# Row loads a step ahead, the readout's scratch in another buffer, and modulation sums on ScalarE in a two-layer hybrid block

## The chip, the core and the metric

The kernel runs on one core of a Trainium2 chip. The metric is the device time of one execution in microseconds. PE is the matrix engine, ACT the scalar engine, DVE the vector engine, POOL the GpSimd engine, SP the engine whose queue issues most of the DMAs.

## What is computed

Two layers over 768 tokens (256 of context, 512 latent), model width 1024. In each layer a conditioning vector gives shift, scale and gate by one product with `ada_w`. The normalised input goes through one wide projection `w_in`; three token mixers (a bidirectional RWKV-7 recurrence, a latent attention, a windowed attention) read slices of it, are gated, projected and merged.

```python
def trunk_layer(x, xc, c, c_ctx, ada_w, ada_b, norm_g, w_in, ...):
    mod = jax.nn.silu(c) @ ada_w + ada_b
    mod_c = jax.nn.silu(c_ctx) @ ada_w + ada_b
    ...
    h = rms_norm(x, norm_g) * (1.0 + scale) + shift
    za, ga, zb, gb, zc, gc, zg = jnp.split(h @ w_in, list(IN_CUTS), axis=-1)
    ...
    ya, yac = rwkv7_branch(za, zac, ...)
...
def rwkv7_scan(r, decay, k, v, kk, a, s0, reverse):
    def step(S, inp):
        r_t, w_t, k_t, v_t, kk_t, a_t = inp
        sa = jnp.einsum('bhvk,bhk->bhv', S, kk_t)
        S = (S * w_t[:, :, None, :] - sa[..., None] * (kk_t * a_t)[:, :, None, :]
             + v_t[..., None] * k_t[:, :, None, :])
        return S, jnp.einsum('bhvk,bhk->bhv', S, r_t)
...
def rwkv7_readout(y, r, v, k_dir, r_k, gn_g, gn_b, dtype):
    mu = jnp.mean(y, axis=-1, keepdims=True)
    var = jnp.mean(jnp.square(y - mu), axis=-1, keepdims=True)
    yn = ((y - mu) * lax.rsqrt(var + A_GN_EPS)).reshape(B, T, BRANCH_WIDTH) * gn_g + gn_b
    ...
```

## The kernel before

**The recurrence.** Time is cut into 12 chunks of 64 tokens; 8 heads times 2 directions run together. For chunk i, `rwkv_scores` (L619) loads from DRAM the update rows `BK` (3 buffers) and `AR` (4 buffers) and the values `UV` (4 buffers), multiplies them on PE (`scps`), masks the products on DVE into `AR` and `TR` (L656, L658), and transposes `BK` on PE. `rwkv_step` (L719) applies one chunk to the state: `Rp`, `Up`, `Sp`, `Yp` on PE, with copies and sums on ACT and DVE between them (`UV`, `So`, `yo`).

**The inversion.** For each group of four chunks, `rwkv_inverse` (L668) inverts the unit triangular 64 by 64 blocks. Four loads bring `TT` (L674, L675; one buffer). DVE transposes it into `inv` (L681), POOL writes a mask into `YB` (L684), then 30 pairs of DVE instructions solve the 32 by 32 halves (L690, L692), each pair using the result of the one before, and two more transposes (L695, L696) end the part on DVE. Only then can PE do the off-diagonal products `zp` and `yp`. There are three inversions to a layer. The first has to be done before chunk 0; the second and third run beside the chunks of the group ahead of them.

**The readout** (L578) normalises finished tokens. Its scratch `ro` has six planes of 256 columns and the tag `AR`, so it takes one of the four `AR` buffers for as long as it lasts. The squares go to planes 4 and 5 in turn.

**The modulation.** `ada` (L227) multiplies the conditioning vectors by blocks of `ada_w` into a PSUM bank `modps`. DVE copies the bank into `row` (L269), PE adds the four partial rows with `sum4` back into the same bank, and DVE adds the bias into `mod` (L277 or L280). Blocks with a weight pool of their own are 512 wide and come at the very start; the other 16 blocks are 256 wide and are spread over layer 0: 4 for layer 0's gate, 12 for layer 1.

**Fillers.** Between the steps of the recurrence the function `pace` puts pieces of other work on PE: projections of `w_in` (`g`) and the `ada` blocks. A projection's weights `wf` are loaded by SP (L165), cast by ACT into `wh` (L168), and POOL makes the rest `wl` (L169); its result in PSUM is finished by ACT (tanh into `st`, L791) and, for a gate projection, by DVE (L793), and SP stores it to `gd` (L795).

**What sets the order.** A list scheduler gives every engine its order when the program is built; each engine then runs its instructions strictly in that order, and SP issues its DMAs in that order too. Priorities are set by `band`. Inside `in_line` PE's order is the order in which the code was written, so PE's order in the recurrence is by hand; the orders of SP, DVE, ACT and POOL come from the scheduler. In `rwkv` (L521) the scores of chunks 0 and 1 and the loads of the first inversion are put in first; step i then puts in the scores of chunk i+2, loads and all.

Of the kernel before, what the change touches and what calls it, by code (L numbers as in the profile page):

```python
# [19 lines left out]
P = 128  # L20
# [40 lines left out]
def build(tc, A, out):  # L61
# [165 lines left out]
    def ada(l, pp, mod, parts, pool=None):  # L227
# [30 lines left out]
        for i_, (q, h) in enumerate((q, h) for q in parts for h in range(512 // n)):  # L258
            ps = bank(i_)

            for k0 in range(0, KT, 4):
                with band(SERVE):
                    ws = four(q, h, k0)
                    for i in range(4):
                        mm(ps[32 * i:32 * i + 32], sc2[:, k0 + i, :], ws[i], start=(k0 == 0), stop=(k0 + 4 == KT),
                           skip_group_check=True)
                yield
            row = spool.tile([P, T], F32, tag="st", name="row", bufs=2)
            V.tensor_copy(row[:, 0:n], ps)  # L269
            nf = n // P  # L270
            pt = ps[:, 0:2 * nf].rearrange("p (f c) -> p f c", c=2)
            for i in range(nf):
                mm(pt[:, i, :], row[:, i * P:(i + 1) * P], C["sum4"])
            if q < 4:
                m, b = (a.rearrange("p (s f) c -> p s f c", s=2)[:, h:h + nf // 2, 2 * q:2 * q + 2]
                        for a in (mod[:, 0:16], pp[:, o:o + 16].unsqueeze(2)))
                V.tensor_tensor(m, pt.rearrange("p (s f) c -> p s f c", s=nf // 2), b.to_broadcast([P, nf // 2, 2, 2]), ALU.add)  # L277
            else:
                f = 4 * q + 2 * h
                V.tensor_tensor(mod[:, f:f + nf], pt, pp[:, o + f:o + f + nf].unsqueeze(2).to_broadcast([P, nf, 2]), ALU.add)  # L280

# [239 lines left out]
    def rwkv(l, D, last, DL, B, pace, zlast):  # L521

        with tc.tile_pool(name="rw", bufs=1, reuse_waits="tile") as rp:
            yo = rp.tile([P, 4, T], F32, name="yo")
            st = {"seen": set(), "S": None}
            parts, YB = {}, {}

            def scores(i):
                if i < NCH:
                    parts[i] = yield from rwkv_scores(l, last, rp, i)  # L530

# [9 lines left out]

            with band(B + 1):
                rest(scores(0), scores(1))
                ahead = invert(0)
# [4 lines left out]
            with band(B + 1), in_line():  # L549
# [3 lines left out]
                for i in range(NCH):  # L553
                    if i % NS == 0:
# [4 lines left out]
                        with band(B + 2):  # L559
                            for _ in range(3):  # L560
                                next(ahead, None)
                    nxt = scores(i + 2)
                    step = rwkv_step(l, last, i, yo, st, DL, rp, parts.pop(i), YB[i // NS])
# [14 lines left out]
    def readout(l, D, rp, yo, part):  # L578
# [9 lines left out]

        tmp = rp.tile([P, 6, 256], F32, tag="AR", name="ro", bufs=4)
        def spread(p):  # L590
            ps = psum_bcast(256)
            mm(ps, bones, tmp[:, 4 + p % 2])
            V.tensor_scalar(tmp[:, p], ps, 1.0 / 64, None, ALU.mult)

        for p in range(4):
# [3 lines left out]
            S.copy(y, like(ps, y))  # L599
            S.activation(like(tmp[:, 4 + p % 2], y), y, AF.Square)  # L600
            if p:
# [16 lines left out]

    def rwkv_scores(l, last, rp, i):  # L619

        has_r = i >= 4 or not last
        AR = rp.tile([P, 8, 3, 64], F32, tag="AR", name="AR", bufs=4)
        BK = rp.tile([P, 8, 2, 64], F32, tag="BK", name="BK", bufs=3)
        UV = rp.tile([P, 2, 8, 64], F32, tag="UV", name="UV", bufs=4)
        DMA.dma_start(BK[EV], bk_d[l][EV, i])
# [6 lines left out]
        else:  # L632
            for par, rows in enumerate(halves):
                DMA.dma_start(AR[rows, :, 2 * par], ar_d[l][rows, i, :, 0])
        DMA.dma_start(UV[OD, 0], v_d[l][:, i, 0])
        DMA.dma_start(UV[EV, 1], v_d[l][:, i, 1])

# [1065 lines left out]
```

## Time and profile before

| | us |
|---|---|
| median of 3 runs | 2326.8 |
| lowest and highest run | 2323.66, 2328.07 |
| the profiled execution, its own time | 2325.92 |
| its span | 2324.2 |
| PE busy | 2080.5 (90%) |
| DVE, ACT, POOL busy | 1271.3, 920.2, 787.7 |
| mean granted clock of PE | 0.956 |

Layer 0's recurrence lies between about 286 and 670 us of the span, layer 1's between about 1574 and 1885 us. PE is the busiest engine by far, so the reading starts from the gaps of PE: how long each is, and which engine's or DMA's work ended it. A "releaser" is the work that ended last before the waiting instruction started.

### The profile page before, as it was taken

Reading aid. Unit: us, or ns where it says so; the run is one execution under the profiler, and the core shown is the slowest. Engines: PE = TensorE matmul, PEld = TensorE weight load, DVE = VectorE, ACT = ScalarE, POOL = GpSimd, SP = SyncE. Lnnn points to the kernel's source line nnn. Section 1 sums busy time; section 2 is a strip of 40 time slices with the busy share of each in tenths; the row PEclk is TensorE's granted clock in tenths of the full one; section 3 lists DMA queues with packets and bytes.
Section 4 is the critical chain, followed back from the end, with each engine's and each line's share of the span. In section 5 each row is a group of like instructions: output and inputs, shape, how many; then the busy total and the mean of one; then the engine's idle time right before and its main releaser. Section 6 shows DMA issues by size and latency. Waiting matters only on the chain. (4 is left out here: it accounts for less than half of the span.)

```text
span 2324.2 us, 42281 instructions
## 1 busy us (share of the span) xinstructions
PE 2080.5 (90%) x16648; PEld 1631.0 (70%) x16648; DVE 1271.3 (55%) x2342; ACT 920.2 (40%) x1694; POOL 787.7 (34%) x646
## 2 busy tenths in 40 slices
PE   6988899888998899989699998889878998998989
PEld 2866677676887777777488877668657876666767
DVE  4467315648335777337537255742668357674742
ACT  3454311233345343354332245543333455444422
POOL 0223112111122444444362323334211145455663
PEclk9999899899999999999899999999989999999999
DMA  7146666554333111531273413567555262215264
GB/s 253 55 138 176 201 197 189 143 144 127 84 107 102 64 46 55 163 109 52 61 232 127 147 62 92 173 201 196 146 121 123 77 215 92 74 51 177 82 195 140
DMA packets 321222, 301.61 MB, mean 130 GB/s; under 512 B 111744, under 2 KB 234368, under 8 KB 321024
## 3 DMA queue, kind: packets, MB, share of 16 engines
q1 hardware_dynamic: 303216, 269.29, 39.0%
q10 hardware_dynamic: 17808, 29.63, 4.0%
q8 instruction: 131, 2.15, 0.4%
q14 instruction: 67, 0.55, 0.1%
HBM read 207.34 MB, written 91.49 MB: 129 GB/s over the span
## 5 line engine op out<-in xcount | busy, mean ns | idle before, releaser
L169 POOL TENSOR_TENSOR wl<-wf,wh 128x512 fp32r<-128x512 f32 x316 | 439.7, 1393 | 1129.4 <-ACT wh L168 1068.6
L157 PE MATMUL g<-hh,wh 128*128 128x512 f32 (+1 forms) x1264 | 468.8, 371 | 11.2 <-DVE st L793 6.4
L157 PE MATMUL g<-hh,wl 128*128 128x512 f32 (+1 forms) x1264 | 455.0, 360 | 8.9 <-POOL wl L169 8.8
L157 PE MATMUL g<-hl,wh 128*128 128x512 f32 (+1 forms) x1264 | 453.1, 358 | 0.0
L168 ACT CAST wh<-wf 128x512 fp32r<-128x512 f32 x316 | 195.1, 619 | 422.2 <-PE g L157 190.0
L157 PEld LDWEIGHTS g<-hh,wh 128*128 128x128 f32 x1264 | 249.8, 198 | 59.2 <-issue 10.4
L157 PEld LDWEIGHTS g<-hh,wl 128*128 128x128 f32 x1264 | 249.1, 197 | 45.4 <-POOL wl L169 10.5
L157 PEld LDWEIGHTS g<-hl,wh 128*128 128x128 f32 x1264 | 249.5, 197 | 33.9 <-issue 4.4
L924 ACT ACTIVATE pe<-stp 128x256 f32<-128x256 f32 (+2 forms) x224 | 114.4, 522 | 173.3 <-PE stp L157 166.6
L928 POOL TENSOR_TENSOR acc<-acc,pe 128x512 f32<-128x512 f32 (+2 forms) x128 | 143.0, 1117 | 106.0 <-ACT pe L924 89.6
L895 DVE TENSOR_REDUCE mx<-mps 128x1 f32<-128x384 f32 (+2 forms) x256 | 123.4, 532 | 29.9 <-PE mps L157 28.9
L157 PE MATMUL g<-yh,wh 128*128 128x512 f32 (+1 forms) x224 | 81.0, 365 | 25.9 <-ACT yh L1387 22.1
L157 PE MATMUL yps<-pe,vh 128*64 128x256 f32 (+1 forms) x704 | 97.1, 382 | 0.0
L949 DVE RECIPROCAL rec<-sps 128x256 f32<-128x256 f32 (+1 forms) x48 | 71.4, 1489 | 44.7 <-PE sps L157 44.1
L656 DVE TENSOR_TENSOR AR<-scps,cst 64x256 f32<-64x256 f32 x96 | 40.1, 418 | 89.8 <-PE scps L157 88.6
L157 PE MATMUL gc<-hh,wh 128*128 128x512 f32 x192 | 78.9, 411 | 10.1 <-DVE rT L363 5.6
L157 PE MATMUL g<-yl,wh 128*128 128x512 f32 (+1 forms) x224 | 81.6, 366 | 3.1 <-POOL yl L1388 3.1
L157 PE MATMUL g<-yh,wl 128*128 128x512 f32 (+1 forms) x224 | 79.3, 357 | 0.0
L157 PE MATMUL gc<-hl,wh 128*128 128x512 f32 x192 | 78.3, 408 | 0.0
L928 POOL TENSOR_TENSOR acc<-pe 128x512 f32<-128x512 f32 (+1 forms) x48 | 53.6, 1116 | 70.8 <-ACT pe L924 67.4
L157 PE MATMUL scps<-AR,BK 64*128 64x128 f32 (+1 forms) x768 | 63.6, 294 | 15.5 <-DMA AR<-ard 13.5
L157 PE MATMUL gc<-hh,wl 128*128 128x512 f32 x192 | 76.5, 399 | 0.0
(392 smaller groups left out, 4293.3 us busy)
## 6 DMA issues: line engine op xcount, KB each, us to landing
wf<-w_in SPq DMA_DIRECT2D x163, 256.0 KB, 2.9
wf<-ada_w SPq DMA_DIRECT2D x84, 256.0 KB, 4.2
wf<-w_in ACTq DMA_DIRECT2D x77, 256.0 KB, 3.1
bkd<-bk SPq DMA_DIRECT2D x16, 768.0 KB, 5.8
zt<-thzg SPq DMA_DIRECT2D x48, 256.0 KB, 3.2
wf<-w_bo SPq DMA_DIRECT2D x40, 256.0 KB, 3.1
thzg<-st SPq DMA_DIRECT2D x24, 384.0 KB, 2.3
vd<-t SPq DMA_DIRECT2D x64, 96.0 KB, 2.4
```

The source lines that it names most:

```text
L157: queued(TE.matmul(o, l, r, start=start, stop=stop, **kw))
L168: S.copy(wh, w32)
L169: eng.tensor_tensor(wl, w32, wh.bitcast(F32), ALU.subtract)
L656: V.tensor_tensor(AR[oth, pds, 2 * par, :], ps[oth, :, a0:a0 + 64], msk("ms", oth), ALU.mult)
L895: V.tensor_reduce(mx, ps, AX.X, ALU.max)
L924: S.activation(e, st, AF.Exp, scale=scale)
L928: G.tensor_tensor(acc, keep.pop(0, acc), e, ALU.add)
L949: V.reciprocal(rec, sps)
```

## The change

Three edits.

1. The loads of `BK` and `AR` move out of `rwkv_scores` into a function `rwkv_rows`. Rows of chunks 0, 1 and 2 are put in before the first scores and before the first inversion's loads; step i puts in the rows of chunk i+3, while the loads of `UV` and the scores stay with chunk i+2.
2. The readout's scratch has four planes instead of six and the tag `BK` (3 buffers) instead of `AR`; the squares are written into the plane that is later overwritten by their mean.
3. In `ada`, for the 16 narrow blocks, `row` is copied by ACT, and the bias is added by two ACT instructions of 128x2 instead of one DVE instruction of 128x4.

```diff
             row = spool.tile([P, T], F32, tag="st", name="row", bufs=2)
-            V.tensor_copy(row[:, 0:n], ps)
+            (V.tensor_copy if pool else S.copy)(row[:, 0:n], ps)
...
-                f = 4 * q + 2 * h
-                V.tensor_tensor(mod[:, f:f + nf], pt, pp[:, o + f:o + f + nf].unsqueeze(2).to_broadcast([P, nf, 2]), ALU.add)
+                f = 8 * h + 2 * q if q < 4 else 4 * q + 2 * h
+                for i in range(nf):
+                    S.activation(mod[:, f + i, :], pt[:, i, :], AF.Identity, bias=pp[:, o + f + i:o + f + i + 1])
...
-            parts, YB = {}, {}
+            parts, YB, rows_ = {}, {}, {}
+
+            def rows(i):
+                if i < NCH:
+                    rows_[i] = rwkv_rows(l, last, rp, i)
...
-                    parts[i] = yield from rwkv_scores(l, last, rp, i)
+                    parts[i] = yield from rwkv_scores(l, last, rp, i, *rows_.pop(i))
...
             with band(B + 1):
+                for i in range(3):
+                    rows(i)
                 rest(scores(0), scores(1))
                 ahead = invert(0)
...
+                    rows(i + 3)
                     nxt = scores(i + 2)
...
-        tmp = rp.tile([P, 6, 256], F32, tag="AR", name="ro", bufs=4)
+        tmp = rp.tile([P, 4, 256], F32, tag="BK", name="ro", bufs=3)
+
         def spread(p):
             ps = psum_bcast(256)
-            mm(ps, bones, tmp[:, 4 + p % 2])
+            mm(ps, bones, tmp[:, p])
             V.tensor_scalar(tmp[:, p], ps, 1.0 / 64, None, ALU.mult)
...
-            S.activation(like(tmp[:, 4 + p % 2], y), y, AF.Square)
+            S.activation(like(tmp[:, p], y), y, AF.Square)
...
-    def rwkv_scores(l, last, rp, i):
+    def rwkv_rows(l, last, rp, i):
...
+        return AR, BK
+
+    def rwkv_scores(l, last, rp, i, AR, BK):
+
+        has_r = i >= 4 or not last
+        UV = rp.tile([P, 2, 8, 64], F32, tag="UV", name="UV", bufs=4)
         DMA.dma_start(UV[OD, 0], v_d[l][:, i, 0])
         DMA.dma_start(UV[EV, 1], v_d[l][:, i, 1])
```

In the changed kernel the lines of the inversion are L689 and L690 (loads of `TT`), L696 (first transpose), L705 and L707 (the pairs), L710 and L711 (last transposes); `st` is finished on DVE at L808, stored at L810. PE's order in the recurrence is the same as before. Three places where the other orders are not:

DVE at the first inversion of layer 0, before. The first transpose follows two instructions of `ada`:

```order
L269 COPY row_3129<-modps_2497 128x256
L277 TENSOR_TENSOR mod1_162<-modps_2497,pp_150 128x4
L681 STREAM_TRANSPOSE inv_2796<-TT_2791 128x1024
L686 MEMSET YB_2790 128x32
L690 TENSOR_TENSOR inv_2796<-inv_2796,YB_2790 128x30
L692 TENSOR_TENSOR YB_2790<-YB_2790,inv_2796 128x30
L690 TENSOR_TENSOR inv_2796<-inv_2796,YB_2790 128x58
```

Further on in the same inversion, before, other work stands between the pairs, here the last `st` that PE's projection needs before `zp`:

```order
L269 COPY row_3429<-modps_2497 128x256
L690 TENSOR_TENSOR inv_2796<-inv_2796,YB_2790 128x84
L793 SCALAR_TENSOR_TENSOR st_3272<-st_3272,g_3273 128x512
L692 TENSOR_TENSOR YB_2790<-YB_2790,inv_2796 128x28x3
L690 TENSOR_TENSOR inv_2796<-inv_2796,YB_2790 128x58
L692 TENSOR_TENSOR YB_2790<-YB_2790,inv_2796 128x29x2
```

DVE at the first inversion of layer 0, after (three of the four `st` instructions that stand ahead of it are shown):

```order
L808 SCALAR_TENSOR_TENSOR st_3200<-st_3200,g_3201 128x512
L808 SCALAR_TENSOR_TENSOR st_3290<-st_3290,g_3292 128x256
L808 SCALAR_TENSOR_TENSOR st_3290<-st_3290,g_3291 128x512
L696 STREAM_TRANSPOSE inv_2809<-TT_2804 128x1024
L701 MEMSET YB_2803 128x32
L705 TENSOR_TENSOR inv_2809<-inv_2809,YB_2803 128x30
L707 TENSOR_TENSOR YB_2803<-YB_2803,inv_2809 128x30
```

All four instructions on `st_3200` and `st_3290`, the counterparts of `st_3183` and `st_3272`, moved ahead of the first transpose; the 60 instructions of the pairs and the two transposes now follow it with nothing but a memset of their own among them.

SP's queue, the last two of the four loads of `TT`, before:

```order
L674 DMA TT_2791<-ttd0_130 32x8x256
L254 DMA wf_3135<-ada_w 128x2x256 [waits DMAHW4_49,PE_49]
L165 DMA wf_3142<-w_in 128x512 [waits DMAHW5_49,PE_49]
L254 DMA wf_3172<-ada_w 128x2x256 [waits DMAHW6_49,DMAHW3_49,Pool_49]
L675 DMA TT_2791<-ttd0_130 32x32x32
```

SP's queue, the last two of these loads, after (`gd` is where a gate projection is stored):

```order
L689 DMA TT_2804<-ttd0_130 32x8x256
L810 DMA gd0_119<-st_3200 128x768 [waits DVE_49]
L254 DMA wf_3368<-ada_w 128x2x256 [waits DMAHW5_49,Pool_49]
L165 DMA wf_3383<-w_in 128x512 [waits DMAHW3_49,DMAHW2_49,PE_49]
L254 DMA wf_3454<-ada_w 128x2x256 [waits DMAHW4_49,PE_49]
L254 DMA wf_3455<-ada_w 128x2x256 [waits DMAHW6_49,PE_49]
L165 DMA wf_3462<-w_in 128x512 [waits DMAHW1_49,PE_49]
L690 DMA TT_2804<-ttd0_130 32x32x32
```

The last load of `TT` moved from behind the weight load `wf_3142` to behind `wf_3462`, six loads of `w_in` later, because the rows of chunk 2 and the values of chunks 0 and 1 now stand ahead of all four.

DVE at the first inversion of layer 1, before:

```order
L793 SCALAR_TENSOR_TENSOR st<-st,g 128x512
L681 STREAM_TRANSPOSE inv<-TT 128x1024
L686 MEMSET YB 128x32
L690 TENSOR_TENSOR inv<-inv,YB 128x30
L692 TENSOR_TENSOR YB<-YB,inv 128x30
```

and after:

```order
L808 SCALAR_TENSOR_TENSOR st<-st,g 128x512 x2
L696 STREAM_TRANSPOSE inv<-TT 128x1024
L808 SCALAR_TENSOR_TENSOR st<-st,g 128x512
L701 MEMSET YB 128x32
L705 TENSOR_TENSOR inv<-inv,YB 128x30
```

Here two of the three `st` moved: the second ahead of the transpose, the third between the transpose and the pairs.

## Rows read from the trace of the kernel before

**Rows 1.** the page: its first line.
```profile
span 2324.2 us, 42281 instructions
```

**Rows 2.** PE waits, 286 to 580 us: total us, times, longest.
```profile
PE scps L157 <- DMA AR<-ard: 13.5, 3, 7.2
PE modps L157 <- DVE mod L280: 6.6, 3, 6.1
```

**Rows 3.** timeline of PE: start, duration, instruction, [idle before <-releaser].
```profile
443.81 0.46 PE L157 MATMUL scps<-AR,BK 64*128 64x128 f32 x2 [3.58 <-DMA AR<-ard]
447.03 2.04 PE L157 MATMUL scps<-AR,BK 64*128 64x128 f32 x14 [2.76 <-DMA AR<-ard]
...
474.40 1.08 PE L157 MATMUL modps<-wf,sc 128*32 128x256 f32 x8 [6.06 <-DVE mod L280]
...
491.98 1.20 PE L157 MATMUL zp<-inv,TT 32*32 32x32 f32 x64
```

**Rows 4.** timeline of PE, 536 to 580 us.
```profile
567.19 2.04 PE L157 MATMUL scps<-AR,BK 64*128 64x128 f32 x14 [7.19 <-DMA AR<-ard]
```

**Rows 5.** timeline of DVE, 345 to 425 us.
```profile
373.04 1.98 DVE L681 STREAM_TRANSPOSE inv<-TT 128x1024 f32<-128x1024 f32 x1
...
377.91 0.27 DVE L690 TENSOR_TENSOR inv<-inv,YB 128x108 f32<-128x108 f32 x1
378.22 1.25 DVE L692 TENSOR_TENSOR YB<-YB,inv 128x108 f32<-128x108 f32 x1
...
404.68 0.67 DVE L793 SCALAR_TENSOR_TENSOR st<-st,g 128x512 f32<-128x512 f32 x1
```

**Rows 6.** timeline of PE, 395 to 425 us.
```profile
405.41 0.50 PE L157 MATMUL g<-hh,wh 128*128 128x512 f32 x1 [1.70 <-DVE st L793]
...
409.90 1.20 PE L157 MATMUL zp<-inv,TT 32*32 32x32 f32 x64 [2.39 <-DVE inv L696]
```

**Rows 7.** one stretch: length, busy PE, PEld, DVE, ACT, POOL, then PE's clock.
```profile
445.30:452.10 6.80, 5.07 (x23) 4.39 (x24) 6.25 (x17) 0.38 (x1) 0.00 (x0) 0.50 1.14 207
```

**Rows 8.** timeline of SP's queue, the loads of TT and a weight load.
```profile
364.20 0.56 SPq L675 DMA_DIRECT2D TT<-ttd  x1
...
398.18 0.34 SPq L165 DMA_DIRECT2D wf<-w_in  x1
```

**Rows 9.** landing of the DMAs that load TT.
```profile
DMA to landing us min/median/max: 3.3/4.2/5.9
```

**Rows 10.** timeline of ACT, 396 to 420 us.
```profile
402.65 0.59 ACT L791 ACTIVATE st<-g 128x512 f32<-128x512 f32 x1
```

**Rows 11.** DVE busy on tile `inv` alone: window, length, busy.
```profile
373.00:410.00 37.00, 28.45 (x62) 1.00 0.66 201
437.00:476.00 39.00, 24.97 (x62) 0.87 0.61 133
...
1679.00:1720.00 41.00, 23.27 (x62) 0.86 0.69 149
```

**Rows 12.** groups of DVE, 373 to 409.8 us: busy, mean | idle.
```profile
L692 DVE TENSOR_TENSOR YB<-YB,inv 128x30 f32<-128x30 f32 (+14 forms) x30 | 13.4, 447 | 0.9
L690 DVE TENSOR_TENSOR inv<-inv,YB 128x30 f32<-128x30 f32 (+14 forms) x30 | 11.8, 394 | 2.2 <-issue 1.4
...
L695 DVE STREAM_TRANSPOSE YB<-YB 128x1024 f32<-128x1024 f32 x1 | 1.9, 1928 | 0.0
```

**Rows 13.** groups of DVE, 437.3 to 475.6 us.
```profile
L656 DVE TENSOR_TENSOR AR<-scps,cst 64x256 f32<-64x256 f32 x6 | 2.5, 416 | 0.1
...
L742 DVE COPY UV<-Up 64x512 f32<-64x512 f32 x1 | 0.7, 696 | 0.0
```

**Rows 14.** timeline of DVE, 1606 to 1632 us, layer 1.
```profile
1619.44 0.15 DVE L690 TENSOR_TENSOR inv<-inv,YB 128x30 f32<-128x30 f32 x1 [2.28 <-issue]
```

**Rows 15.** timeline of ACT, 1596 to 1660 us, layer 1.
```profile
1624.78 0.59 ACT L791 ACTIVATE st<-g 128x512 f32<-128x512 f32 x1
```

**Rows 16.** PE waits, 1570 to 1890 us, layer 1.
```profile
PE zp L157 <- DVE inv L696: 12.7, 2, 10.7
```

More of the change, by code (lines that the diff above doesn't have):

```diff
@@ L273, in ada @@
                 mm(pt[:, i, :], row[:, i * P:(i + 1) * P], C["sum4"])
-            if q < 4:
+            if pool:
                 m, b = (a.rearrange("p (s f) c -> p s f c", s=2)[:, h:h + nf // 2, 2 * q:2 * q + 2]
@@ L623, in rwkv_scores @@
         BK = rp.tile([P, 8, 2, 64], F32, tag="BK", name="BK", bufs=3)
-        UV = rp.tile([P, 2, 8, 64], F32, tag="UV", name="UV", bufs=4)
         DMA.dma_start(BK[EV], bk_d[l][EV, i])
```

## The prediction

> **What bounds the kernel now.** The profiled execution took 2325.92 us, of which 2324.2 us are the span [rows 1]; the median of the runs shown, 2326.8 us, is 0.9 us above it. PE is the busiest engine, and its order in the recurrence stays as it is, so I read the waits of PE first. In layer 0's recurrence, the row loads are what it waits for longest: 13.5 us in three waits for `AR`, and 6.6 us for a modulation sum on DVE, 6.1 us of it in one wait [rows 2]. These are what the change touches. Then I read the timeline of PE around each wait. Step 3's scores wait 3.58 and 2.76 us for `AR`, a `modps` matmul waits 6.06 us for `mod` [rows 3], and step 8's scores wait 7.19 us [rows 4]. Last I read the other side, DVE around the first inversion: its first transpose starts at 373.04 us [rows 5], its last one ends just ahead of `zp`, which PE starts at 409.90 us after a wait of only 2.39 us, with 1.70 us for an `st` shortly before [rows 6]. So DVE's first inversion, some 37 us long, already ends on PE's path: any later start of it is paid by PE.
>
> A wait of that length also costs clock. From 445.3 to 452.1 us, right after the step 3 waits, PE's granted clock is 0.50, the lower of its two levels, 1.2 GHz [rows 7]; at the higher one the 5.07 us of work in it would have taken half, so the loss is about 2.5 us. I count the same for the `mod` wait, and 2.2 us for step 8.
>
> **The change part by part.**
>
> *What it removes.* Step 3's rows are now in the queue ahead of that step's weight loads and before the values of steps 2 and 3; they are issued while PE still waits for the first inversion. That takes away 3.58 + 2.76 + 2.5 = 8.8 us. The `mod` wait goes since ACT, free at that time, does the sum: 6.06 + 2.5 = 8.6 us. In step 8 the slot of `AR` came free late because the readout's scratch held one of four buffers, so that chunk 8 had to take chunk 5's; now it takes chunk 4's, and the load goes out some 20 us sooner: 7.19 + 2.2 = 9.4 us. Together 26.8 us, if nothing else becomes late.
>
> *The first inversion of layer 0: +24.2 us.* The rows of chunk 2 stand ahead of the loads of `TT` in SP's queue. These loads slip backwards past weight loads that wait for PE; the last of the four moves from 364.20 us to right behind the weight load that SP issued at 398.18 us [rows 8]. With a median of 4.2 us to land [rows 9] it is there at about 402.9 us. The scheduler then placed DVE's transpose behind all four `st` instructions, the last of which needs a tanh that ACT does from 402.65 to 403.24 us [rows 10]; at 0.67 us for it [rows 5] the transpose starts at about 404.0 us instead of 373.04. From there it is a chain on DVE with nothing in between: the instructions on `inv`, 23.27 to 28.45 us in the inversions of before, with 24.97 us in the second [rows 11], 1.9 us for the transpose that only touches `YB`, and 0.9 + 2.2 us of idle time between them, 1.4 of it the wait for POOL's mask [rows 12]. I take 24.97, since only few casts of weights will run on POOL beside it: 24.97 + 1.9 + 3.1 = 30.0 us, end at 434.0. PE's `zp` stands where it stood, at the same `g`, so it starts at 434.1 instead of 409.90: +24.2 us (bounds 22.5 and 27.7 by the two ends of rows 11). Nothing covers this, since PE's order is by hand and the fillers behind `zp` can't pass it. The two small waits ahead of `zp`, 1.70 and 2.39 us, are within the figure. The clock after the wait is low before, too, so I add nothing for that.
>
> Some of the DVE instructions took a microsecond longer than their size calls for: 1.25 us for a `YB` update beside 0.27 us for the `inv` product of the same size [rows 5]. The Trainium skill, SBUF — State Buffer, "Who interferes with whom", says that a DVE instruction with two SBUF inputs contends with a GpSimd instruction that reads SBUF; the pairs have two such inputs, and POOL's subtraction for `wl` reads two. By that rule, with PE standing still and POOL soon out of casts, the inversion would run at the 23.27 us end, 404.0 + 28.3 = 432.3 us, and the term would be 22.5 instead of 24.2; the trace of before shows the slow instructions, not what the stall will do to POOL.
>
> *The second inversion takes back part of the gain.* It starts on DVE at about 436.5 us on the clock of before (all that follows `zp` is moved by the same 24 us). Its last transpose now stands behind all of step 2: 16 mask instructions at 0.416 us and 12 others (`UV`, `So`, `st`, `yo`) between 0.42 and 0.70 us, for which I take 0.6 [rows 13], stand among its own: 6.7 + 7.2 + 30.0 = 43.9 us, end at 480.4. PE starts the `zp` for it at 491.98 us before [rows 3], and without the waits of step 3 and `mod` (17.4 us) it would be there at 474.6. So it waits 5.9 us, and loses 2.5 us more to the low clock: of 17.4 us, 9.0 stay. The bounds are 5 us (DVE has gaps of its own) and 17.4 us (the inversion starts sooner).
>
> *Step 8.* The third inversion is now spread among steps 4 to 6, and DVE is full there; I take 1 us off: -8.4 us, bounds -5 and -9.4.
>
> *Layer 1: +5 us.* There is no `ada` left, and hardly a wait for rows. But the order of DVE moves here, too: the pairs of the first inversion start at 1619.44 us [rows 14], and now stand behind a third `st`, whose tanh ends at 1625.37 us [rows 15]. At 0.67 us for that `st` [rows 5] they start at 1626.1: 6.7 us later, less two `st` (1.3 us) that no longer stand among them. PE waits there for DVE already; in its waits for the last transposes it lost 12.7 us, one of them 10.7 us [rows 16]. So about 5 us come through. Bounds: -3 us (the waits behind it shrink by as much) and +10 us (other DVE work of the attention gets in among the second inversion, and is paid too).
>
> *ACT instead of DVE for the modulation.* 16 copies and 32 small sums on an engine that is idle for more than half of the span; apart from the `mod` wait above nobody waits for them. Zero.
>
> **Sum.** 24.2 - 9.0 - 8.4 + 5.0 = +11.8 us; 2325.9 + 11.8 = 2337.7, and with the 0.9 us to the median 2338.6, say 2338 us.
>
> **The rivals.** A difference of 0.2%, 4.7 us, is about what a measurement of this kernel can tell from no change.
>
> *Faster (0.13).* The point that decides is whether the second inversion is done when PE arrives. If DVE ends it by 474.6 us, all 26.8 us are gained; with the first inversion at its lower bound and layer 1 at -3 the sum is 22.5 - 26.8 - 3 = -7.3, 2319.5 us. For it: the three waits removed are plain to see. Against: DVE has 43.9 us of work in 38. The Trainium skill, Trainium Kernel Development and Optimization, "Best Practices", advises to double-buffer so that DMA and compute overlap; taken alone, the loads ahead of time would give the full -26.8 us, 2300 us. The trace says that the loads passed over (`TT`) are on the path, too.
>
> *No change (0.20).* Full gains, the first inversion at the lower bound, layer 1 at +5: 22.5 - 26.8 + 5 = +0.7, about 2327.5 us.
>
> *The rows still come late (0.10).* If SP's queue is held so long by weight loads that wait for POOL or PE that `AR` is not there in step 3 or 8, those terms fall away: 24.2 - 3 + 0 + 5 = +26, with part of step 8 some +18, 2345 us. Against: the row loads of step 3 stand ahead of the next weight load that waits for PE.
>
> *Worse (0.12).* POOL gets in the way of the first inversion (27.7), of the first gain half is lost (-4.5 stay), step 8 gives its lower bound (-5), layer 1 is at +10: +28, 2355 us.
>
> My forecast has 0.45. Slower by over 0.2% is the forecast and the last two, 0.67; within 0.2% 0.20; faster by over 0.2% 0.13. The range for 8 in 10 goes from 2321 us (part of the faster case out) to 2351 us (part of the worst out).
>
> **What would show it.** In layer 0 the first inversion's transpose at about 404 us, and a wait of PE of some 27 us in front of the first `zp`. No wait for `AR` in steps 3 and 8, none for `mod`. PE waits some 6 us for DVE at the second `zp`, at about 505 us of the new span. In layer 1, the pairs of the first inversion start some 6 us later against its first `st`. I am wrong if the first transpose starts before 400 us, if PE has other work in front of `zp`, or if the gap at `zp` is there but the time is below 2322: then the gains are larger than I count.

## The result, and the profile of the changed kernel

The changed kernel is slower: a median of 2342.23 us in 16 runs (2330.49 to 2349.95), against 2327.32 us of the kernel before in 16 runs beside it (2319.93 to 2332.75). The ratio is 1.0062, with a 95% interval of 1.0049 to 1.0076, that is +14.4 us; +11.8 us were forecast.

| | before, us | after, us |
|---|---|---|
| median | 2327.32 | 2342.23 |
| profiled execution, its own time | 2325.92 | 2349.95 |
| its span | 2324.2 | 2347.9 |
| PE busy | 2080.5 | 2090.9 |
| mean granted clock of PE | 0.956 | 0.945 |

The profiled execution of after is its longest run, 7.7 us above its median, and that of before 1.4 us below its own. So the two spans differ by 23.7 us, 9 us more than the ratio gives. I take places and waits from the traces, and what the change and its parts are worth from ratios. In the experiments below each ratio stands against the runs of the kernel before on the same chip.

The page of after begins with its span:

```profile
span 2347.9 us, 42275 instructions
```

The waits of PE in 286 to 580 us of after (total, times, longest) answer to [rows 2]:

```profile
PE zp L157 <- DVE inv L711: 26.9, 1, 26.9
...
PE modps L157 <- ACT mod L281: 2.7, 4, 1.2
PE scps L157 <- DVE TR L673: 2.2, 1, 2.2
```

The three waits for `AR` and the one of 6.1 us for `mod` are gone, and a single wait of 26.9 us, which was 2.39 us [rows 6], takes their place. How it comes about stands on three engines. SP's queue, the last load of `TT`; then DVE, from the last `st` to the last transpose (columns: start, duration, instruction, [idle before <-releaser]); then PE, the `zp` of the first inversion:

```profile
398.45 0.57 SPq L690 DMA_DIRECT2D TT<-ttd  x1
```

```profile
400.45 0.69 DVE L808 SCALAR_TENSOR_TENSOR st<-st,g 128x512 f32<-128x512 f32 x1 [3.28 <-ACT st L806]
401.68 2.02 DVE L696 STREAM_TRANSPOSE inv<-TT 128x1024 f32<-128x1024 f32 x1 [0.54 <-DMA TT<-ttd]
...
406.59 0.27 DVE L705 TENSOR_TENSOR inv<-inv,YB 128x108 f32<-128x108 f32 x1
406.89 0.27 DVE L707 TENSOR_TENSOR YB<-YB,inv 128x108 f32<-128x108 f32 x1
...
428.95 1.25 DVE L711 STREAM_TRANSPOSE inv<-YB 128x1024 f32<-128x1024 f32 x1
```

```profile
430.34 1.92 PE L157 MATMUL zp<-inv,TT 32*32 32x32 f32 x64 [26.88 <-DVE inv L711]
...
447.98 1.15 PE L157 MATMUL Rp<-UV,AR 128*64 128x64 f32 x32
```

The load is issued at 398.45 us, 34.25 us later than before [rows 8]. DVE's transpose waits for it until 401.68 us, and DVE ends the inversion at 430.20 us. PE has been idle since 403.46 us. After it has gone on, the clock is low for some time yet. By stretch (length, busy time of PE, PEld, DVE, ACT, POOL, then PE's granted clock), in after:

```profile
406.60:430.30 23.70, 0.00 (x0) 0.00 (x0) 21.70 (x56) 1.27 (x2) 0.00 (x0) 0.50 0.50 77
430.30:447.60 17.30, 16.75 (x274) 13.92 (x276) 1.44 (x4) 5.01 (x10) 3.17 (x3) 0.50 0.34 85
```

and in before, the low stretch behind its first `zp`, and the `Rp` that follows it on PE:

```profile
411.10:418.00 6.90, 6.65 (x58) 5.14 (x59) 0.49 (x3) 1.16 (x2) 0.75 (x1) 0.51 0.24 78
```

```profile
423.12 1.15 PE L157 MATMUL Rp<-UV,AR 128*64 128x64 f32 x32
```

What the later steps give back is seen on DVE, at the first and the last transpose of the second inversion, and on PE, at the `zp` that waits for it and around step 8:

```profile
460.04 2.00 DVE L696 STREAM_TRANSPOSE inv<-TT 128x1024 f32<-128x1024 f32 x1
...
501.62 1.22 DVE L711 STREAM_TRANSPOSE inv<-YB 128x1024 f32<-128x1024 f32 x1
```

```profile
502.99 1.20 PE L157 MATMUL zp<-inv,TT 32*32 32x32 f32 x64
```

```profile
569.60 1.16 PE L157 MATMUL scps<-AR,BK 64*128 64x128 f32 x16
...
576.69 1.49 PE L157 MATMUL scps<-AR,BK 64*128 64x128 f32 x14 [2.16 <-DVE TR L673]
...
588.85 1.15 PE L157 MATMUL Rp<-UV,AR 128*64 128x64 f32 x32 [1.07 <-ACT UV L742]
```

The last of these in before:

```profile
583.17 1.15 PE L157 MATMUL Rp<-UV,AR 128*64 128x64 f32 x32
```

The second `zp` has no wait, but DVE ends that inversion at 502.84 us, only 0.15 us ahead of it. Against 491.98 us [rows 3] it is 11.0 us late. The scores that waited 7.19 us for `AR` [rows 4] are the 16 at 569.60 us, without a wait. The next ones wait 2.16 us for DVE, and `Rp` 1.07 us; that `Rp` was at 583.17 us before, so 5.7 us of shift are left.

Layer 1 is the other place. PE at its first inversion, all waits in 1654 to 1672 us of after:

```profile
1654.26 0.50 PE L157 MATMUL g<-hh,wh 128*128 128x512 f32 x1 [2.80 <-DVE st L808]
...
1659.65 0.47 PE L160 MATMUL gqm<-cst,raw 128*128 128x128 f32 x1 [3.04 <-DMA raw<-zbd]
1662.38 0.48 PE L160 MATMUL gqm<-cst,raw 128*128 128x128 f32 x1 [2.26 <-DMA raw<-zbd]
1665.01 0.69 PE L160 MATMUL gqm<-cst,raw 128*128 128x128 f32 x2 [2.15 <-ACT x L1231]
1670.28 1.92 PE L157 MATMUL zp<-inv,TT 32*32 32x32 f32 x64 [4.59 <-DVE inv L711]
```

and the same place of before, 1640 to 1672 us:

```profile
1647.14 0.50 PE L157 MATMUL g<-hh,wh 128*128 128x512 f32 x1 [1.19 <-DVE st L793]
...
1655.55 1.92 PE L157 MATMUL zp<-inv,TT 32*32 32x32 f32 x64 [6.07 <-issue]
```

`gqm` are matmuls of the attention; in after, two pieces of them stand ahead of `zp` in PE's order, and they wait for the loads of `raw` and for ACT. From 7.1 us at the `g` the shift grows to 14.7 us at `zp`. The `gqm` are not what makes `zp` late: the last of them is over at 1665.70 us, and what PE then waits for is DVE's last transpose. DVE's first `st`, first pair and last transpose there, in after:

```profile
1624.20 0.69 DVE L808 SCALAR_TENSOR_TENSOR st<-st,g 128x512 f32<-128x512 f32 x1 [14.64 <-ACT st L806]
...
1637.27 0.15 DVE L705 TENSOR_TENSOR inv<-inv,YB 128x30 f32<-128x30 f32 x1 [1.50 <-issue]
...
1668.98 1.25 DVE L711 STREAM_TRANSPOSE inv<-YB 128x1024 f32<-128x1024 f32 x1
```

and the first `st` and the last transpose of before, whose first pair is at 1619.44 us [rows 14]:

```profile
1614.52 0.69 DVE L793 SCALAR_TENSOR_TENSOR st<-st,g 128x512 f32<-128x512 f32 x1 [12.40 <-ACT st L791]
...
1654.23 1.22 DVE L696 STREAM_TRANSPOSE inv<-YB 128x1024 f32<-128x1024 f32 x1
```

DVE ends at 1670.23 us in after and `zp` starts at 1670.28; in before it ends at 1655.45 and `zp` starts at 1655.55. So the 6.07 us of before, put down to `issue` (no releaser that the profile shows), are a wait for DVE, too. DVE works without a gap from the first pair on, and its small instructions for the `gqm` take some 0.6 us of that; so without the `gqm` PE would have waited for DVE until about the same time. What made DVE late is worked out below, under layer 1.

### The profile page after: what moved, and what is told of

It reads as the page before. It is cut to its first block, busy times and chain, and to the rows that moved or that the text cites. A ratio compares the mean times of both kernels' runs of the same rounds, so it can differ in the third digit from the quotient of the medians.

```text
span 2347.9 us, 42275 instructions
## 1 busy us (share of the span) xinstructions
PE 2090.9 (89%) x16648; PEld 1640.3 (70%) x16648; DVE 1256.9 (54%) x2310; ACT 931.0 (40%) x1742; POOL 788.2 (34%) x646
## 5 line engine op out<-in xcount | busy, mean ns | idle before, releaser
L806 ACT ACTIVATE st<-g 128x256 f32<-128x256 f32 (+1 forms) x108 | 56.5, 523 | 44.4 <-PE g L157 43.3
```

The source lines that it names most:

```text
L806: S.activation(t[:, sl], p, AF.Tanh, scale=0.5)
```

## The experiments

Twelve kernels were run. The expectations compare with about 2327 us; the kernel before took 2330 to 2332 us in these runs, so a time T of an expectation is to be held against the ratio times 2327.

**1. The rows of chunk 2 behind the loads of `TT`.** Of the changed kernel, only this is put back.

```diff
-                for i in range(3):
+                for i in range(2):
                     rows(i)
                 rest(scores(0), scores(1))
                 ahead = invert(0)
                 for _ in range(4):
                     next(ahead)
+                rows(2)
```

> The changed kernel with one thing moved: the rows of chunk 2 are put in behind the four loads of TT of the first inversion, not ahead of them; all else as in the changed kernel. In DVE's order the first transposes of both layers stand ahead of the st instructions again. Theory (the queue order of TT and with it DVE's order cost the time, and the gains are real): the wait of PE of 27 us ahead of the first zp of layer 0 falls to under 5 us, first zp within 4 us of 410, no wait for mod or for AR in step 8, layer 1's first zp no longer late; time 2308 to 2318 us. Rival 1 (what ACT took over, or the scratch in BK, costs the time): the zp wait may go, but the time stays above 2330. Rival 2 (the gains were only there because DVE was early or PE late; with the first inversion in time the waits come back elsewhere): 2322 to 2330.

Measured: 0.9971 [0.9954, 0.9989], 2320.3 us by the ratio; the changed kernel stands at 1.0062. The waits of PE, 390 to 600 us:

```profile
PE zp L157 <- DVE inv L712: 7.6, 2, 4.6
```

The first `zp` waits 4.6 us instead of 26.9, and there is no wait for `AR` here either. So the whole loss, 0.9% or 21 us, hangs on the place of one group of rows in SP's queue in each layer. It is the rows of chunk 2 alone: the values of chunks 0 and 1, which I named beside them as the reason, stand ahead of `TT` here as in the kernel before (issued from 314.73 to 339.88 us there, the first `TT` at 340.40). But the gain over before is 0.3%, and not the 0.4 to 0.8% that I expected: the second `zp` waits 3.0 us, and after the 4.6 us PE's clock is low from 409.5 to 426.6 us (experiment 4 has the same). By the trace layer 0's recurrence gained more: from its first `bkp` (PE's transposes of `BK`) to its last `Rp` it takes 321.2 us, 333.0 in before and 336.2 in after. How much of such a gain reaches the end of the kernel is taken up under "Left open".

**2. The loads of `TT` ahead of the first scores.** Of the changed kernel, the inversion's loads go ahead of the values of chunks 0 and 1 as well, and the rows of chunk 2 behind.

```diff
-                for i in range(3):
+                for i in range(2):
                     rows(i)
-                rest(scores(0), scores(1))
                 ahead = invert(0)
-                for _ in range(4):
+                next(ahead)
+                rest(scores(0), scores(1))
+                for _ in range(3):
                     next(ahead)
+                rows(2)
```

> As the run before, but the loads of TT stand ahead of the scores of chunks 0 and 1, too. Theory: the first transpose is no longer bound by its loads but by its place in DVE's order; as DVE ends the inversion some us before PE comes to zp, little more than in the run before: 2305 to 2318 us. Rival 1 (earlier TT loads delay the scores' rows, which PE then waits for): 2318 to 2330, with a new wait for AR or UV ahead of step 0.

Measured: 0.9935 [0.9911, 0.9959], 2311.9 us. No wait at the first `zp`, but look at the others, PE's waits in 390 to 600 us, and ACT in 440 to 470 us:

```profile
PE modps L157 <- ACT mod L281: 7.8, 4, 5.6
PE scps L157 <- DMA AR<-ard: 7.2, 2, 3.8
```

```profile
463.73 1.04 ACT L715 COPY YB<-YB 32x1024 f32<-32x1024 f32 x1 [5.95 <-DVE YB L712]
464.79 0.41 ACT L281 ACTIVATE mod<-modps,pp 128x2 f32<-128x2 f32 x2
```

With PE on time, the rows of step 3 are late again (7.2 us in two waits), and the modulation sum is late on ACT as it was on DVE: it stands behind a copy of `YB` that waits 5.95 us for the second inversion on DVE. So in the changed kernel these waits are gone not by the edits alone: behind the 26.9 us everything was on time.

**3. The modulation back on DVE,** the rest as changed.

```diff
-            (V.tensor_copy if pool else S.copy)(row[:, 0:n], ps)
+            V.tensor_copy(row[:, 0:n], ps)
...
-                for i in range(nf):
-                    S.activation(mod[:, f + i, :], pt[:, i, :], AF.Identity, bias=pp[:, o + f + i:o + f + i + 1])
+                V.tensor_tensor(mod[:, f:f + nf], pt, pp[:, o + f:o + f + nf].unsqueeze(2).to_broadcast([P, nf, 2]), ALU.add)
```

> The changed kernel with the modulation on DVE as before (rows ahead and scratch in BK kept). TT's loads and DVE's first transpose stand as late as in the changed kernel. Theory: the wait ahead of the first zp stays at 25 to 32 us, since it comes from edit 1 alone, and the modulation wait comes back in part: 2340 to 2352 us. Rival 1 (what ACT took over costs the time): faster than the changed kernel by more than 5 us, below 2337.

Measured: 1.0080 [1.0050, 1.0111], 2345.6 us. The wait at `zp` is 27.2 us, and the wait for `mod` is back with 4.4 us. So the modulation has no part in the long wait. Its worth, 1.0080 against 1.0062, is within the intervals.

**4. Only the modulation on ACT,** the kernel before else: edit 3 alone.

> The kernel before with the modulation's copy and sums on ACT, nothing else. Theory: the 6.06 us wait for mod and the slow clock behind it go, the waits for AR in steps 3 and 8 stay: 8.6 us less, 2316 to 2322 us. Rival 1 (ACT is needed for the weight casts and the copies cost as much): 2325 us or more.

Measured: 0.9997 [0.9981, 1.0014]. This missed. The wait for `mod` fell from 6.06 to 1.2 us, but the time of the whole kernel did not fall by anything that can be measured. PE's waits in 390 to 600 us, and a stretch behind the first `zp`, which here starts at 405.11 us:

```profile
PE scps L157 <- DMA AR<-ard: 11.8, 2, 8.9
PE zp L157 <- DVE inv L697: 4.6, 1, 4.6
PE modps L157 <- ACT mod L281: 2.7, 4, 1.2
```

```profile
405.10:421.30 16.20, 15.69 (x234) 12.83 (x236) 1.44 (x4) 4.91 (x10) 3.17 (x3) 0.50 0.29 75
```

The `zp` waits 4.6 us (2.39 before), the `AR` of step 8 8.9 us (7.19), and the clock is low until 421.3 us, 16 us from `zp` on. In before it is low there from 411.1 to 418.0 us, 6.8 us, so 9.4 us more are at half speed, a cost of 4.7 us if PE is busy. The longer wait at `zp` is no loss: PE came sooner, and `zp` is 4.8 us earlier than in before (405.11 against 409.90 us). At the next `Rp` only 0.8 us of that are left, behind the wait for `mod` it is 9.2 us, and at the last `Rp` of layer 0 7.3 us. As 1.7 us of it stood at the first `bkp` already, this recurrence is 5.7 us shorter in the trace, of the 8.6 us that I expected. In the whole kernel's ratio it is not seen.

**5. Only the readout's scratch in `BK`,** the kernel before else: edit 2 alone.

> The kernel before with the readout's scratch in four planes of tag BK, nothing else. Theory: the 7.19 us wait for AR in step 8 and the 2.2 us of slow clock go, all else stays: 8 to 10 us less, 2316 to 2322 us. Rival 1 (what was late there only moves to the third inversion's zp or to the next BK load): 2325 us or more.

Measured: 0.9995 [0.9978, 1.0012], a miss like the last. PE's waits in 390 to 600 us:

```profile
PE scps L157 <- DMA UV<-vd: 3.5, 1, 3.5
PE scps L157 <- DMA AR<-ard: 3.5, 1, 3.5
...
PE scps L157 <- DVE TR L659: 1.7, 1, 1.7
```

The 7.19 us at step 8 are gone, and a wait of 1.7 us for DVE came in; what is left of `AR` is step 3's, where `AR` and `UV` together take 7.0 us (6.3 before). `Rp`, too, waits 2.4 us for `UV` where it waited 0.3. That leaves 7.19 - 1.7 - 0.7 - 2.1 = 2.7 us of gain by the waits, less than the interval of 4 us to each side can show. From the first `bkp` to the last `Rp` layer 0's recurrence is 7.2 us shorter in the trace, as the clock is low for less of it, too (mean 0.96, 0.94 in before); that is near the 8 to 10 us expected, but again it is not in the ratio.

**6. and 11. The rows behind `TT` in one layer only.** Experiment 1's edit, in layer 1 alone (6) and in layer 0 alone (11).

```diff
-                for i in range(3):
+                for i in range(2 if l == 1 else 3):
                     rows(i)
...
+                if l == 1:
+                    rows(2)
```

> The changed kernel with the rows of chunk 2 behind TT's loads in layer 1 only; layer 0 as in the changed kernel. Theory (the first inversion of layer 1 pays 5 us in its own right): the 27 us wait in layer 0 stays, the first zp of layer 1 waits 6 us as before, and layer 1's recurrence loses 2 to 4 us instead of 9: 2334 to 2338 us, 4 to 8 less than the changed kernel. Rival 1 (layer 1's loss follows from layer 0's): same time as the changed kernel, within 3 us.

> The changed kernel with the rows of chunk 2 behind TT's loads in layer 0 only; layer 1 as in the changed kernel. Theory (layer 1's loss of some 10 us stands by itself: the matmuls gqm of the last token tile come ahead of zp and wait for their own loads): 8 to 12 us more than the run with rows behind TT in both layers, ratio 1.0005 to 1.0025, with waits for raw ahead of layer 1's first zp. Rival 1 (it was a consequence of layer 0's lateness): ratio 0.996 to 0.998.

Measured: 6 gave 1.0018 [1.0001, 1.0035], and 11 gave 0.9994 [0.9973, 1.0015]. PE in layer 1, waits in 1590 to 1735 us, of 6 and then of 11:

```profile
PE zp L157 <- DVE inv L713: 10.8, 1, 10.8
PE zp L157 <- issue: 6.0, 1, 6.0
```

```profile
PE zp L157 <- DVE inv L713: 10.7, 2, 6.1
PE gqm L160 <- ACT x L1233: 4.6, 2, 2.7
PE gqm L160 <- DMA raw<-zbd: 4.3, 2, 2.7
```

In 6 layer 0 has its 26.7 us wait, and layer 1 is as before; in 11 it is the other way round. So what layer 1 pays does not come from layer 0 being late, but from the rows of chunk 2 ahead of its own `TT`. In 11 DVE's pairs of the first inversion stand behind the third `st` again, in 6 behind the first as in before. Its size is 1.0062 - 1.0018 = 0.44%, 10 us, by 6, and 0.9994 - 0.9971 = 0.23%, 5 us, by 11 against 1; the intervals don't part the two, and the second does not exclude zero. Both runs came out faster than expected (2331.2 us by the ratio for 2334 to 2338; 0.9994 for 1.0005 to 1.0025). The traces agree better: from the first `bkp` to the last `Rp` layer 1's recurrence takes 258.6 us in before, 260.3 to 261.7 us in experiments 1, 4, 5, 6 and 9, and 268.0 and 267.4 us in after and in 3, some 6 to 9 us more. Layer 0 pays the rest.

**7. and 8. More ahead.** To experiment 2, 7 adds the rows of chunk 3 up front (the loop puts in `rows(i + 3)` from i = 1 on), and 8 moves the copies of `YB` from ACT to POOL besides.

```diff
-            S.copy(YB[b0:b0 + 32, :, 32:64], YB[b0:b0 + 32, :, 0:32])
+            G.tensor_copy(YB[b0:b0 + 32, :, 32:64], YB[b0:b0 + 32, :, 0:32])
```

> The run with TT's loads first, and the rows of chunk 3 put in ahead of the recurrence, too, with those of chunk 2. Theory: in the changed kernel the step 3 wait went because PE stood still at zp while SP went on; with PE on time it is back (3.41 and 3.77 us in the run with TT first), and only an earlier place in the queue takes it away: no wait for AR in step 3. But the wait for mod (5.61 us there, released by DVE's last transpose through ACT's copies of YB) is set by DVE's second inversion and grows by what PE arrives sooner: the time falls by 0 to 5 us only against the run with TT first, 2311 to 2317. Rival 1 (the waits are independent): 10 to 13 us less, 2303 to 2306.

> As the run before, with the two copies of YB behind the last but one transpose on POOL instead of ACT, so that ACT's modulation sums no longer stand behind DVE's second inversion. Theory: neither the wait for AR in step 3 nor the one for mod; PE comes to the second zp some 17 us sooner and may wait there for DVE: 10 to 17 us less than the run with TT first, 2299 to 2306. Rival 1 (POOL, waiting for DVE's transpose, delays the weight casts behind it, or DVE is slowed by POOL's copies): 2310 or more.

Measured: 0.9927 [0.9902, 0.9951] and 0.9941 [0.9920, 0.9962]; experiment 2 was 0.9935. Step 3 no longer waits for rows in 7, but step 4 does, 3.4 us, and the second `zp` waits 2.6 us; in 8 these are 4.0 and 2.4 us. The waits moved, the time did not. The mechanism that I expected in 7, a longer wait for `mod`, did not come: it is 1.2 us. 8 missed: 2313 us by the ratio, where 2299 to 2306 were expected.

**9. Edits 2 and 3 without edit 1.** The kernel before, with the readout's scratch in `BK` and the modulation on ACT; rows as before.

> The kernel before with the modulation on ACT and the readout's scratch in BK; row loads where they were. It differs from the run with the rows of chunk 2 behind TT by the row loads alone. Each of the two edits by itself changed nothing that could be measured (ratios 0.9997 and 0.9995). Theory: the two waits (for mod, and for AR in step 8) go, 2 to 8 us less, ratio 0.9965 to 0.999, and the row loads a step ahead add nothing while the first inversion is on time. Rival 1 (the loads a step ahead are what made the run with rows behind TT 0.3% faster): ratio 0.999 to 1.001.

Measured: 0.9969 [0.9957, 0.9982], as experiment 1 (0.9971), though step 3 still waits 3.1 us for `AR` here and not there. So rows a step ahead are worth nothing that can be measured, with the first inversion where it was in before; the intervals leave room for some 5 us either way.

**10. One line of the kernel before.** Only the loads of `TT` go ahead of the first scores; none of the three edits.

```diff
-                rest(scores(0), scores(1))
                 ahead = invert(0)
-                for _ in range(4):
+                next(ahead)
+                rest(scores(0), scores(1))
+                for _ in range(3):
                     next(ahead)
```

> The kernel before with nothing changed but the place of the first inversion's TT loads, ahead of the scores of chunks 0 and 1. Theory: the first inversion ends before PE needs it, the waits of 1.70 and 2.39 us ahead of zp go; in layer 1 the 6.07 us wait shrinks to 1.4 as it did with TT first and all three edits; 8 to 12 us with the slow clock behind these waits: ratio 0.995 to 0.9965, that is most of what the run with TT first gained. Rival 1 (TT first pays only with the other edits): ratio 0.998 or more.

Measured: 0.9936 [0.9916, 0.9957], 2312.1 us, as experiment 2, faster than both kernels, and more than the 0.35 to 0.5% that I expected. PE's waits in 390 to 600 us, then those in 1590 to 1735 us:

```profile
PE scps L157 <- DMA AR<-ard: 12.3, 2, 8.7
PE modps L157 <- DVE mod L280: 5.0, 3, 4.5
```

```profile
PE zp L157 <- DVE inv L697: 10.8, 1, 10.8
```

The waits for which the change was made are all there, 12.3 and 5.0 us, yet it is as fast as experiment 2 and within the interval of 7, the fastest. What it takes away is the wait at the first `zp` of both layers (2.4 and 6.1 us before), the 1.7 us for `st` ahead of the one in layer 0, and there the low clock behind it (6.8 us before).

**12. `TT` late in the kernel before.** Only layer 0's loads of `TT` get a lower priority, so that they fall behind the rows of chunk 2 and the `BK` of chunk 3.

```diff
                 ahead = invert(0)
-                for _ in range(4):
+                if l == 1:
+                    for _ in range(4):
+                        next(ahead)
+            if l == 0:
+                with band(B + 6):
                     next(ahead)
+                with band(B + 1):
+                    for _ in range(3):
+                        next(ahead)
```

> The kernel before with nothing changed but the place of the TT loads of layer 0's first inversion, now behind the rows of chunks 2 and 3 in SP's queue, so that DVE's first transpose stands behind the four st instructions as in the changed kernel (the loads come some us later even than there). None of the three edits is in it. Theory (the place of TT makes the whole loss in layer 0, and PE's standing still is what makes the waits of step 3 and for mod go): PE waits 28 to 35 us at the first zp, no wait for AR in step 3, the mod wait under 3 us, the wait for AR in step 8 stays; ratio 1.005 to 1.009. Rival 1 (the edits themselves cost the time): ratio 1.000 to 1.002 with a shorter wait. Rival 2 (the edits took away the step 3 and mod waits in the changed kernel): these waits stay here, ratio 1.011 or more.

Measured: 1.0135 [1.0092, 1.0178], 2358 us, above what I expected. DVE's first transpose, then PE's waits in 390 to 600 us:

```profile
411.78 1.90 DVE L688 STREAM_TRANSPOSE inv<-TT 128x1024 f32<-128x1024 f32 x1 [12.10 <-DMA TT<-ttd]
```

```profile
PE zp L157 <- DVE inv L703: 38.4, 1, 38.4
PE scps L157 <- DMA AR<-ard: 7.2, 1, 7.2
PE modps L157 <- DVE mod L280: 5.0, 3, 4.4
```

The loads went further back than in the changed kernel, so `zp` waits 38.4 us. That the place of these loads alone makes the loss is borne out. The two waits of step 3 for `AR` are gone here without edit 1, while the 7.2 us of step 8 and 4.4 us for `mod` stay: a long stall hides step 3's, and only the edits remove the other two.

Not run: rows ahead with the readout left in the `AR` buffers. Then the rows three ahead and the readout would want the same four buffers.

## Why the prediction was right, point by point

The range, the sign and the case held: 2342 us against 2338, and the change is slower because the loads of `TT` slip back. Its terms were right in sum rather than one by one, and that the sum came so near is in part luck.

*The first inversion, +24.2 us forecast, +20.4 measured* (430.34 against 409.90 us). The mechanism was right: the last load behind the weight load, the transpose behind the last `st`, nothing to cover PE. Two sizes were off. The load went out at 398.45 us, as said, but landed after 3.2 us and not after the median of 4.2 [rows 9], and the last `st` was over at 401.14 us, since PE had come to its projection some 3 us earlier. So the transpose began at 401.68 and not at 404.0 us. And the chain on DVE took 28.5 us (401.68 to 430.20), not 30.0: the pair that took 0.27 and 1.25 us in before [rows 5] took 0.27 and 0.27 us at the same size, with POOL idle after its mask, and the chain is near its lower bound of 28.3 us. The Trainium skill, SBUF — State Buffer, "Who interferes with whom", says that a DVE instruction with two SBUF inputs contends with a GpSimd instruction that reads SBUF. No such instruction ran beside the chain, which by that rule would take 28.3 us; the trace agrees. The upper bound was set too low: layer 1's first inversion of before, which [rows 11] leaves out, has 31.72 us on `inv`.

*The clock behind that wait, 0 forecast, some +4.5 us measured.* This step failed. I took it to be as low as before, where it is low for 6.8 us of the work behind `zp`; in after it is 0.50 for 17.3 us, nearly all of it busy. At the next `Rp`, 447.98 us against 423.12 us before, the shift has grown from 20.4 to 24.9 us.

*The second inversion, 9.0 us back forecast, 13.9 measured* (24.9 to 11.0 us). The working held better than the term. DVE took 42.8 us for that inversion (460.04 to 502.84), 43.9 were forecast, and it ends just ahead of the second `zp`. The wait of some 6 us that I named as a sign did not come, as PE had lost 4.5 us to the clock on its way there: most of what I counted as a wait behind the step was paid ahead of it. So this term and the two before it belong together: 24.2 - 9.0 = +15.2 us at the second `zp` were forecast and +11.0 measured; 3.8 us of the difference are the first inversion's. The reason given for the gain, though, was too simple. That step 3's rows come on time, I put down to edit 1; experiment 12 has the same without it, and in experiment 2 the wait is back with it. In the changed kernel both work.

*Step 8, 8.4 us back forecast, 5.3 measured* (11.0 to 5.7 us). The wait for `AR` went, but 2.16 us for DVE and 1.07 us at `Rp` came in, as the lower bound of 5 us allowed. Alone, this edit is not to be measured (experiment 5).

*Layer 0 together*: 20.4 + 4.5 - 13.9 - 5.3 = +5.7 us in the trace, where the sum said 24.2 - 9.0 - 8.4 = +6.8. The errors nearly cancelled. 2.5 us of the 5.7 stood before the recurrence, at the first `bkp` (320.96 against 318.50 us).

*Layer 1, +5 us forecast, 5 to 10 measured by the ratios, 9.4 in the trace* (a shift of 9.7 us at its first `bkp`, 19.1 us at its last `Rp`). At the first inversion the working held. In before the first pair starts 4.9 us behind the start of the first `st`, in after 13.1 us, with two more `st` between: 8.1 us later, where 6.7 were forecast. From there to the end of the last transpose DVE takes 33.0 us instead of 36.0, 3.0 us less, where 1.3 were forecast for the two `st` that moved ahead. So 5.1 us come through to `zp`, as the sum said. One reading was wrong: the waits of [rows 16] are those at the second and the third inversion, and the wait at the first was the 6.07 us put down to `issue`. What the sum left out comes behind it. At the second inversion eight instructions of the attention, 3.2 us, stand among DVE's own in after, and two, 0.6 us, in before; DVE takes 42.4 us for it instead of 39.8, and PE waits for its end. I had named this as the reason for the upper bound of +10 us. I had also read PE's order in the recurrence as unchanged. That holds for the part written by hand, not for `gqm`, the attention's matmuls of the last token tile, which the scheduler places. At the first `zp` they stand in time in which PE would have waited for DVE.

*The rivals.* "Faster" hung on a second inversion that is done when PE comes, "no change" on a first one at its lower bound with all gains whole. The second was done, by 0.15 us, and the first came out below its bound (20.4 against 22.5 us), but the gains were 13.9 + 5.3 = 19.2 us and not 26.8, and the clock took 4.5. With one row group moved the change would have been faster: 0.9971 in experiment 1. That PE's three waits were worth 26.8 us "if nothing else becomes late" was the largest error, which the forecast didn't rest on: with `TT` where it was in before, the edits together gave some 7 us (6.7 in experiment 1 with all three, 7.2 in 9 with two), and with `TT` first nothing within some 7 us (2 against 10). "The rows still come late" was wrong. The Trainium skill, Trainium Kernel Development and Optimization, "Best Practices", advises double-buffering, so that DMA and compute overlap. Loads put in ahead cost time here, since they pushed back others in the same queue, and gave nothing to be measured where they didn't (0.9971 in experiment 1 against 0.9969 in 9).

*Left open.* Between the two recurrences the trace of after loses 4.0 us against that of before, and from the end of layer 1's to the end of the kernel another 5 us, both with more of the time at the low clock. As this profiled run is 7.7 us above its median, I don't read it as the change's. The same stretch between the recurrences (last `Rp` of layer 0 to first `bkp` of layer 1) takes 936.9 us in before, and from 937.1 us (experiment 5) to 946.1 us (experiment 2) in others. Each is one traced run, on several chips, so I can't tell whether gains in layer 0's recurrence, 11.8 us in experiment 1 and 5.7 and 7.2 us in 4 and 5, are lost again there by a cause or by chance; the ratios, over many runs, show 0.3% and nothing. The 10 us that experiment 6 gives for layer 1 may hold some of layer 0's clock, which was low for 17 us behind the long wait in after and for 9 us in 6. Nor is it settled whether edits 2 and 3 together give more (0.3%) than each alone (0.05 and 0.03%); the intervals allow that they only add up.

## What to carry to other kernels

When loads are put in ahead of time, ask of the queue that issues them in order which loads they pass: here `TT`, 34 us later, cost more than the rows could give, and the same loads put first gave 0.64%, in one moved line. A wait that vanishes from a profile is no gain while a longer one stands ahead of it; look at it again with that one gone. And a wait taken from PE is not yet time: price it with the next thing that is late, and try it alone.

## What was not expected of the hardware

How long PE's clock stays low after a wait differs much. It was at 0.50 for 6.8 us around the `zp` of before, after waits of 1.70 and 2.39 us, but for 17 us from `zp` on in after, where PE had stood still for 26.9 us, and for 16 to 17 us in experiments 1, 4 and 9, after no more than 4.6 us. In experiment 11 it was 14 us after the same 4.6 us, in experiment 12 14 us after 38.4 us, and in experiments 3 and 6, after 27 us, 9 us. So the length of the wait doesn't tell what the clock behind it costs: two kernels with about the same wait, after and experiment 6, differ by 8 us of low clock in the trace.
